# Storing one cast per element in a row, and reading its source with a step of two

## The chip, the cores and the metric

The kernel runs on one core of a Trainium2 chip. The time is that of the device, in microseconds (us), for one execution of the whole program. Three executions of the kernel before took 877.74, 879.22 and 881.9 us; the median is 879.22 us. A core has five engines that the text names: PE (TensorE, matrix products; PEld is its loading of weights), DVE (VectorE), ACT (ScalarE), POOL (GpSimd) and SP (SyncE, which here only issues transfers from memory).

## The reference, cut to what matters

The program computes four residual layers over a sequence of 256 tokens of width 1024 in 32-bit floats, and a last normalisation. Layer 0 and layer 3 are causal pooling mixers, layer 1 is a gated delta rule, layer 2 is latent attention:

```python
for i in range(DEPTH):                     # DEPTH = 4
    kind, j = i % N_MIXERS, i // N_MIXERS  # N_MIXERS = 3
    h = rmsnorm(x, norm_g[i])
    if kind == 0:
        y = pool_mixer(h, pool_w_in[j], pool_w_grp[j], pool_scale[j], pool_w_out[j])
    elif kind == 1:
        y = gdn_mixer(h, gdn_w_in[j], ...)
    else:
        y = mla_mixer(h, positions, mla_w_in[j], ...)
    x = x + y
return rmsnorm(x, final_g)
```

Every mixer is a few large matrix products (`h @ w_in`, products of the mixer's own, `y @ w_out`) with element-wise work between them. Some 137 MB are read from memory, nearly all of it weights, each read once.

## The kernel before, in words

**Products in three parts.** A 32-bit operand `a` of a product is split into `hi`, which is `a` rounded to the type float32r, and `lo`, which is `a - hi`. The product is then `hi*hi + hi*lo + lo*hi`. For weights, `weights` (L110) does this for one row block of 128 x 512 (called a K-tile here): SP loads two K-tiles at a time into one of three `raw` buffers (512 KB, L117), ACT casts `raw` to `whi` (L135; L139 where a gain is multiplied in), and DVE, or in a few K-tiles of layer 1 POOL, writes `wlo = raw - whi` (L136, L140). The pairs go into a ring of nine. A `raw` buffer is free for the next load when both K-tiles in it have been cast and subtracted. For activations `split_out` (L218) does the same with L225/L227 on ACT and L230/L232 on DVE.

**The alternating order.** A product streams one operand through PE (the moving operand, `rhs`) and keeps the other one in it (`lhsT`). `mm` (L148) reads the moving operand in an alternating order: element 0, element n/2, element 1, element n/2 + 1 and so on over each stretch of n columns (`woven`), and writes its result to consecutive columns (`inorder`). So whatever is to be a moving operand has to be stored such that this order gives the true one: the even columns in the first half of the stretch, the odd ones in the second half. The result is as if nothing had been permuted.

**Who stores in it.** There are two kinds of projections in `project` (L156). With `chan` the weights are `lhsT`; their casts read and write in a row. Without it the activations are `lhsT` and the weights move; these casts are called with `weave` and store in the alternating order. Without `chan` go: the first gate and the first mixing of each pooling layer, the gates of layer 1, the first three column blocks of layer 2, its rotary queries and its values, and all four output projections (`layer_out`, L424: first 512 columns at once, then 512 in two cuts of 256). Also stored in that order are the pooled values `ph`/`pl`, the products `yTh`/`yTl` of pooling and attention, the heads' `qkh`/`qkl`/`qk0` (L1246, L1247; read from PSUM, where PE leaves its results), the queries `kqT` of layer 1 (L768), and two small constants (L701, L1107).

In the kernel before such an instruction walks through its operands so that the source is read in a row and every second element is written half a stretch away:

```python
v, lo, hi = inorder(v, weave), woven(lo, weave), woven(hi, weave)
...
a = nc.scalar.copy(hi, v)                              # L135
b = e.tensor_tensor(out=lo, in0=v, in1=hi.bitcast(F32), op=ALU.subtract)  # L136
```

**What sets the order.** Each engine runs its own list of instructions in order and waits by semaphores. The order in these lists is set when the program is built, by a planner that goes by modelled costs. After the last block of an output projection comes a chain that nothing of the next layer can pass: `x` is added up (L429), squares are summed (L239), POOL works out the norm (L275 to L281, L369), the normalised rows `h` (L376, L381) are turned by PE (L396) and split into `hTh`, `hTl` (L225, L230).

Of the kernel before, what the change touches and what calls it, by code (L numbers as in the profile page):

```python
# [16 lines left out]
P = 128  # L17
# [25 lines left out]
def trunk(ctx: ExitStack, tc: tile.TileContext, x, positions, norm_g, pool_w_in, pool_w_grp,  # L43
# [47 lines left out]
    ready = []  # L91
    held_back = {"free": 0, "after": []}

    def inorder(a, n=P):

        if len(a.shape) == 3 and a.shape[2] != n:
            a = a.rearrange("p h s -> p (h s)")
        if len(a.shape) == 3:
            return a.rearrange("p h (a b) -> p h a b", b=2)
        return a.rearrange("p (g a b) -> p g a b", a=n // 2, b=2)  # L100
# [9 lines left out]
    def weights(src, n, cols, raw=None, pool=(), gain=None, weave=0):  # L110

        if raw is None:
            raw = rawp.tile([P, KU * CW], F32, tag="raw", name="raw")
        m = n * cols
        dst = raw[:, :m]
        if len(src.shape) == 3:
            dma = nc.sync.dma_start(out=dst.rearrange("p (k c) -> p k c", k=n), in_=src)  # L117
        else:
            dst = dst.rearrange("p (k a b) -> p k a b", k=n, a=src.shape[2])
            for k in range(n):  # L120
                dma = nc.sync.dma_start(out=dst[:, k], in_=src[:, k])
        parts = []
        for k in range(n):
            v = raw[:, k * cols:(k + 1) * cols]
            lo = ring.tile([P, CW], F32R, tag="wlo", name="wlo")[:, :cols]
            hi = ring.tile([P, CW], F32R, tag="whi", name="whi")[:, :cols]
            parts.append((hi, lo))
            if weave:
                v, lo, hi = inorder(v, weave), woven(lo, weave), woven(hi, weave)
            held = held_back["free"] <= 0  # L130
            held_back["free"] -= 1
            with later(*(held_back["after"] if held else ())):
                e = nc.gpsimd if k in pool else nc.vector
                if gain is None:
# [3 lines that stand above are left out]
                    g = gain[:, k:k + 1]  # L138
                    a = nc.scalar.activation(hi, v, AF.Copy, scale=g)  # L139
                    b = e.scalar_tensor_tensor(out=lo, in0=v, scalar=g, in1=hi.bitcast(F32),  # L140
                                               op0=ALU.mult, op1=ALU.subtract)
        mark.update(sp=dma.ins, act=a.ins)
        if n - 1 not in pool:
            mark["dve"] = b.ins
        return parts
# [72 lines left out]
    def split_out(*tiles, weave=False):  # L218

        if weave:  # L220
            tiles = [(inorder(ps), [woven(o) for o in parts], scale)
                     for ps, parts, scale in tiles]
        for ps, (hi, lo), scale in tiles:
            if scale is None:
                a = nc.scalar.copy(hi, ps)  # L225
            else:
                a = nc.scalar.activation(hi, ps, AF.Copy, scale=scale)  # L227
        for ps, (hi, lo), scale in tiles:
            if scale is None:
                b = nc.vector.tensor_tensor(out=lo, in0=ps, in1=hi.bitcast(F32), op=ALU.subtract)  # L230
            else:
                b = nc.vector.scalar_tensor_tensor(out=lo, in0=ps, scalar=scale,  # L232
                                                   in1=hi.bitcast(F32), op0=ALU.mult,
                                                   op1=ALU.subtract)
        return [a.ins, b.ins]
# [394 lines left out]
    def gdn_layer(i, j, hT):  # L630
# [67 lines left out]
        ps = bank(aux, "aux")  # L698
        nc.tensor.transpose(ps[:M, :P], Gf, ident)
        grow = workb("grow", P)[:M]  # L700
        nc.vector.tensor_copy(woven(grow), inorder(ps[:M, :P]))  # L701
        d_g = dram.tile([M, P], F32, name="d_g")
        nc.gpsimd.dma_start(out=d_g, in_=grow)
        Gb = [big("Gb", H, P) for _ in range(NT)]
# [50 lines left out]
        def channels(dst, c0, hf, which):  # L755
# [4 lines left out]
            for b in range(2):  # L760
                cv = [worka("cv", S) for _ in range(2)]
                conv(*[(banks[b][:, c * S:(c + 1) * S], (c0 + hf * CW) // P + 2 * b + c, cv[c])
                       for c in range(2)])
                for c in range(2):
                    o, v = dst[hf][:, 2 * b + c, :], cv[c]
                    if which:
                        o, v = woven(o), inorder(v)
                    nc.scalar.activation(o, v, AF.Silu)  # L768
            for c in range(0, 4, 2):
                ps = bank(tps, "tp").rearrange("p (t a s) -> p t a s", a=2, t=NT)  # L770
# [325 lines left out]
    def mla_setup():  # L1096
# [5 lines left out]
        for name, src in (("mask16", cmask), ("turn16", ident)):  # L1102
            MC[name] = const.tile([P, P], BF16, name=name)
            o = MC[name]
            if src is ident:
                o, src = woven(o), inorder(src)
            nc.gpsimd.tensor_copy(o, src)  # L1107

    def mla_layer(i, j, hT):
# [123 lines left out]
        def heads(g):  # L1233
            h0 = g * G8
            for c in range(2):
                for dst, w, e, nk, a in ((qT, mla_w_uq[j], 192, NQ, cqT),
# [5 lines left out]
                    for b in range(2):  # L1242
# [1 line left out]
                        two = slice(2 * b, 2 * b + 2)  # L1244
                        split_out((ps[:, :, a0:], [o[:, two] for o in dst[-1][1]], None),
                                  weave=True)  # L1246
                        nc.vector.tensor_copy(woven(dst[-1][0][:, two]), inorder(ps[:, :, :P]))  # L1247
                banks = project(heads_of(mla_w_ukv[j], 256, h0 + 4 * c, 4, NOPE, P), units(NKV),
                                ckn)
                v.append((tuple(big("v" + x, CW, dt=F32R) for x in "hl"), big("v1", CW)))  # L1250
# [138 lines left out]
```

## Time and profile before

| | |
|---|---|
| three executions, median | 879.22 us (877.74 to 881.9) |
| the profiled execution | 880.5 us, span 878.7 us |
| mean granted PE clock in it | 0.973 |
| PE busy | 820.4 us, 93% of the span |
| DVE busy | 700.8 us, 80% |
| ACT busy | 605.6 us, 69% |
| POOL busy | 168.0 us, 19% |
| read from memory | 137.27 MB, 158 GB/s over the span |

The span runs from the first to the last instruction; the 1.8 us beside it belong to the start and the end of the program. A row of the profile names the line of the kernel, the engine, the operation, the written tile and the tiles read (`whi<-raw`), the shape, how often it ran, its busy time and the mean of one. PE's busy time is modelled from pipelined products: a product of 512 columns is shown with 379 ns although the next one starts some 215 ns later, so gaps shorter than the difference don't show as idle time. A row's shape is the product of its dimensions: a cast that stores in the alternating order and one that stores in a row both read 128x512.

### The profile page before, as it was taken

Reading aid. Unit: us, or ns where it says so; the run is one execution under the profiler, and the core shown is the slowest. Engines: PE = TensorE matmul, PEld = TensorE weight load, DVE = VectorE, ACT = ScalarE, POOL = GpSimd, SP = SyncE. Lnnn points to the kernel's source line nnn. Section 1 sums busy time; section 2 is a strip of 40 time slices with the busy share of each in tenths; the row PEclk is TensorE's granted clock in tenths of the full one; section 3 lists DMA queues with packets and bytes.
Section 4 is the critical chain, followed back from the end, with each engine's and each line's share of the span. In section 5 each row is a group of like instructions: output and inputs, shape, how many; then the busy total and the mean of one; then the engine's idle time right before and its main releaser. Section 6 shows DMA issues by size and latency. Waiting matters only on the chain.

```text
span 878.7 us, 16173 instructions
## 1 busy us (share of the span) xinstructions
PE 820.4 (93%) x5962; PEld 768.5 (87%) x5962; DVE 700.8 (80%) x1156; ACT 605.6 (69%) x997; POOL 168.0 (19%) x296
## 2 busy tenths in 40 slices
PE   8989989889899989999979999999999999899995
PEld 6979978878899878888969999999988879899885
DVE  5799889866788978557867789989988867877894
ACT  7676567868765766567867686777866775566784
POOL 3111100141444992023120112000000210000012
PEclk9999989999999989899999999999999999899999
DMA  6755654646655544303637786752542556565463
GB/s 192 224 169 168 192 168 147 198 135 189 187 154 167 167 129 137 121 17 106 183 103 199 226 202 179 203 153 78 168 144 74 167 148 201 160 197 198 139 195 84
DMA packets 109079, 139.90 MB, mean 159 GB/s; under 512 B 21316, under 2 KB 51208, under 8 KB 109000
## 3 DMA queue, kind: packets, MB, share of 16 engines
q1 hardware_dynamic: 106608, 137.12, 52.3%
q0 software_dynamic: 528, 1.58, 0.7%
q8 instruction: 47, 0.77, 0.4%
q10 hardware_dynamic: 1864, 0.17, 0.2%
q14 instruction: 32, 0.26, 0.1%
HBM read 137.27 MB, written 1.58 MB: 158 GB/s over the span
## 4 chain that ended last, share of the span: by engine, by line
PE 49%; DVE 16%; DMA 10%; ACT 10%; issue 7%; POOL 6%; SPq 1%; DVEq 0%; ACTq 0%; POOLq 0%
PE acc L148 38%; DVE wlo L136 7%; ACT whi L135 5%; DMA raw<-in_pool_w_out_dram 4%; PE aux L148 4%; DMA raw<-in_pool_w_in_dram 3%; POOL Tb L831 3%; POOL pr L827 2%; DVE wlo L140 1%; DVE win L531 1%; DVE yTl L230 1%; ACT whi L139 1%; ACT ph L225 1%; PE aux L787 1%; ACT junk L239 1%
## 5 line engine op out<-in xcount | busy, mean ns | idle before, releaser
L135 ACT CAST whi<-raw 128x512 fp32r<-128x512 f32 (+1 forms) x444 | 368.5, 903 | 139.2 <-PE acc L148 50.9
L136 DVE TENSOR_TENSOR wlo<-raw,whi 128x512 fp32r<-128x512 f32 (+1 forms) x430 | 385.0, 949 | 90.3 <-ACT whi L135 87.6
L148 PE MATMUL acc<-hTh,whi 128*128 128x256 f32 x832 | 232.8, 280 | 3.2 <-ACT gsg L651 2.6
L148 PE MATMUL acc<-hTl,whi 128*128 128x256 f32 x832 | 233.0, 280 | 0.0
L148 PE MATMUL acc<-hTh,wlo 128*128 128x256 f32 x832 | 232.0, 279 | 0.4 <-DVE wlo L140 0.4
L148 PEld LDWEIGHTS acc<-hTh,whi 128*128 128x128 f32 x832 | 162.8, 196 | 4.0 <-ACT gsg L651 2.8
L148 PEld LDWEIGHTS acc<-hTl,whi 128*128 128x128 f32 x832 | 162.7, 196 | 0.3
L148 PEld LDWEIGHTS acc<-hTh,wlo 128*128 128x128 f32 x832 | 162.4, 195 | 0.6 <-DVE wlo L140 0.5
L148 PE MATMUL acc<-wlo,yTh 128*128 128x256 f32 (+1 forms) x384 | 116.5, 320 | 8.4 <-DVE wlo L136 8.2
L148 PE MATMUL acc<-whi,yTh 128*128 128x256 f32 (+1 forms) x384 | 114.9, 321 | 4.4 <-ACT whi L135 3.0
L148 PE MATMUL acc<-whi,yTl 128*128 128x256 f32 (+1 forms) x384 | 90.9, 318 | 0.0
L148 PEld LDWEIGHTS acc<-wlo,yTh 128*128 128x128 f32 x384 | 74.4, 194 | 15.8 <-DVE wlo L136 12.5
L148 PEld LDWEIGHTS acc<-whi,yTh 128*128 128x128 f32 x384 | 74.4, 195 | 9.0 <-ACT whi L135 4.2
L148 PEld LDWEIGHTS acc<-whi,yTl 128*128 128x128 f32 x384 | 64.4, 195 | 3.4
L139 ACT ACTIVATE whi<-raw,gain 128x512 fp32r<-128x512 f32 x64 | 47.5, 790 | 28.8 <-DMA raw<-in_pool_w_in_dram 18.5
L364 POOL TENSOR_TENSOR hg<-x,gain 128x256 f32<-128x256 f32 x16 | 14.7, 931 | 264.5 <-DVE x L429 264.5
L148 PE MATMUL acc<-wlo,hTh 128*128 128x512 f32 (+1 forms) x144 | 55.7, 390 | 3.4 <-DVE wlo L136 1.9
L148 PE MATMUL acc<-whi,hTh 128*128 128x512 f32 (+1 forms) x144 | 53.9, 387 | 4.4 <-ACT hTh L225 1.9
L140 DVE SCALAR_TENSOR_TENSOR wlo<-raw,gain,whi 128x512 fp32r<-128x512 f32 x64 | 49.5, 800 | 9.9 <-ACT whi L139 9.7
L148 PE MATMUL acc<-whi,hTl 128*128 128x512 f32 (+1 forms) x144 | 43.0, 377 | 0.1
L530 POOL COPY win<-u 128x4 f32<-128x4 f32 x8 | 6.3, 790 | 180.8 <-ACT u L524 96.5
L148 PEld LDWEIGHTS acc<-whi,hTh 128*128 128x128 f32 x144 | 28.1, 195 | 9.9 <-ACT hTh L225 4.4
(357 smaller groups left out, 1563.5 us busy)
## 6 DMA issues: line engine op xcount, KB each, us to landing
raw<-in_pool_w_in_dram SPq DMA_DIRECT2D x62, 512.0 KB, 4.3
raw<-in_gdn_w_in_dram SPq DMA_DIRECT2D x48, 512.0 KB, 3.9
raw<-in_pool_w_out_dram SPq DMA_DIRECT2D x32, 512.0 KB, 4.3
raw<-in_mla_w_in_dram SPq DMA_DIRECT2D x24, 512.0 KB, 4.6
raw<-in_mla_w_uq_dram SPq DMA_DIRECT2D x36, 256.0 KB, 3.5
raw<-in_pool_w_grp_dram SPq DMA_DIRECT2D x16, 512.0 KB, 3.9
raw<-in_gdn_w_out_dram SPq DMA_DIRECT2D x16, 512.0 KB, 3.7
raw<-in_mla_w_ukv_dram SPq DMA_DIRECT2D x32, 256.0 KB, 3.5
```

The source lines that it names most:

```text
L135: a = nc.scalar.copy(hi, v)
L136: b = e.tensor_tensor(out=lo, in0=v, in1=hi.bitcast(F32), op=ALU.subtract)
L139: a = nc.scalar.activation(hi, v, AF.Copy, scale=g)
L140: b = e.scalar_tensor_tensor(out=lo, in0=v, scalar=g, in1=hi.bitcast(F32), op0=ALU.mult, op1=ALU.subtract)
L148: return nc.tensor.matmul(inorder(o, n), lhsT=lhs, rhs=woven(rhs, n), start=start, stop=stop)
L225: a = nc.scalar.copy(hi, ps)
L230: b = nc.vector.tensor_tensor(out=lo, in0=ps, in1=hi.bitcast(F32), op=ALU.subtract)
L239: nc.scalar.activation(junk[:, :n], src, AF.Square, scale=scale, accum_out=o)
L364: nc.gpsimd.tensor_tensor(out=self.early[t, a], in0=xs[t][:, sl], in1=self.g[:, sl], op=ALU.mult)
L531: nc.vector.tensor_tensor(out=nxt[:, :, d:], in0=cur[:, :, d:], in1=cur[:, :, :S - d], op=ALU.add)
L827: nc.gpsimd.tensor_tensor(out=pv, op=ALU.mult, in0=Lb[:, r, r + 1:, None].to_broadcast([M * Q, n, c]), in1=Tb[:, r:r + 1, :c].to_broadcast ...
L831: mark["blocks"] = nc.gpsimd.tensor_tensor(out=tv, in0=tv, in1=pv, op=ALU.subtract).ins
```

## The change

Two new views, `parted` and `halves`, take the place of `inorder` and `woven` at every instruction on ACT, DVE and POOL that stores in the alternating order. The same elements go to the same places; only the order in which one instruction walks through them is another. Where it went 0, 1, 2, 3 in the source and 0, n/2, 1, n/2 + 1 in the destination, it now goes 0, 2, 4, ... and then 1, 3, 5, ... in the source and 0, 1, 2, 3, ... in the destination. The second source of a subtraction, `hi`, is walked through like the destination. The views of PE (`mm`), of the lower triangle (L794) and of the copies on POOL at L1197 stay.

```diff
+    def parted(a, n=P):
+        if len(a.shape) == 3 and a.shape[2] != n:
+            a = a.rearrange("p h s -> p (h s)")
+        if len(a.shape) == 3:
+            return a.rearrange("p h (a b) -> p h b a", b=2)
+        return a.rearrange("p (g a b) -> p g b a", a=n // 2, b=2)
+
+    def halves(a, n=P):
+        if len(a.shape) == 3 and a.shape[2] != n:
+            a = a.rearrange("p h s -> p (h s)")
+        if len(a.shape) == 3:
+            return a.rearrange("p h (b a) -> p h b a", b=2)
+        return a.rearrange("p (g b a) -> p g b a", a=n // 2, b=2)
@@ weights
             if weave:
-                v, lo, hi = inorder(v, weave), woven(lo, weave), woven(hi, weave)
+                v, lo, hi = parted(v, weave), halves(lo, weave), halves(hi, weave)
@@ split_out
         if weave:
-            tiles = [(inorder(ps), [woven(o) for o in parts], scale)
+            tiles = [(parted(ps), [halves(o) for o in parts], scale)
                      for ps, parts, scale in tiles]
@@ gdn_layer
-        nc.vector.tensor_copy(woven(grow), inorder(ps[:M, :P]))
+        nc.vector.tensor_copy(halves(grow), parted(ps[:M, :P]))
@@ gdn_layer, channels
                     if which:
-                        o, v = woven(o), inorder(v)
+                        o, v = halves(o), parted(v)
@@ mla_setup
             if src is ident:
-                o, src = woven(o), inorder(src)
+                o, src = halves(o), parted(src)
@@ mla_layer, heads
-                        nc.vector.tensor_copy(woven(dst[-1][0][:, two]), inorder(ps[:, :, :P]))
+                        nc.vector.tensor_copy(halves(dst[-1][0][:, two]), parted(ps[:, :, :P]))
```

In the changed file every line behind the new functions has a number that is 16 higher (L136 is L152, L230 is L246).

How the instructions stand shows best on DVE around the output projection of layer 0. The rows give line, operation, what is written from what, and the dimensions of the walk: `128x256x2` is 128 partitions by 256 pairs of elements that lie half a stretch apart. Before:

```order
L136 TENSOR_TENSOR wlo<-raw,whi 128x256x2
L539 SCALAR_TENSOR_TENSOR p<-win,u 128x1024
L136 TENSOR_TENSOR wlo<-raw,whi 128x256x2 x2
L552 SCALAR_TENSOR_TENSOR y<-aux,colsT,gs 128x256 x4
L230 TENSOR_TENSOR pl<-p,ph 128x8x64x2
L136 TENSOR_TENSOR wlo<-raw,whi 128x256x2
L230 TENSOR_TENSOR yTl_1699<-y,yTh_1698 128x4x64x2 x2
L136 TENSOR_TENSOR wlo<-raw,whi 128x256x2 x7
```

And in the change, at the same place:

```order
L152 TENSOR_TENSOR wlo<-raw,whi 128x512
L555 SCALAR_TENSOR_TENSOR p<-win,u 128x1024
L152 TENSOR_TENSOR wlo<-raw,whi 128x512 x2
L568 SCALAR_TENSOR_TENSOR y<-aux,colsT,gs 128x256 x4
L246 TENSOR_TENSOR pl<-p,ph 128x1024
L152 TENSOR_TENSOR wlo<-raw,whi 128x512
L246 TENSOR_TENSOR yTl_1699<-y,yTh_1698 128x512 x2
L152 TENSOR_TENSOR wlo<-raw,whi 128x512 x7
```

Nothing moved here: the same instructions stand in the same order, and the destination is now one run of 512 or 1024 elements. That holds for the whole lists of DVE, ACT, POOL and SP. The one place that moved is on PE, in layer 1, where the third gate's products (L148) run beside the inversion of the triangular blocks (L919). Before:

```order
L148 MATMUL acc<-wlo,hTh_2249 128x512
L148 MATMUL acc<-whi,hTh_2249 128x512
L919 MATMUL aux<-T,LT 128x64 x8
L148 MATMUL acc<-wlo,hTh_2249 128x512
L148 MATMUL acc<-whi,hTl_2250 128x512 x2
```

And in the change:

```order
L164 MATMUL acc<-whi,hTh_2249 128x512
L935 MATMUL aux<-T,LT 128x64 x8
L164 MATMUL acc<-wlo,hTh_2249 128x512
L164 MATMUL acc<-whi,hTh_2249 128x512
L164 MATMUL acc<-wlo,hTh_2249 128x512
L164 MATMUL acc<-whi,hTl_2250 128x512 x2
```

Two products of the gate stand behind the eight small ones instead of ahead of them.

## The prediction

> **What bounds the kernel now.** I read the page first: busy shares, then the chain that ended last.
>
> ```profile
> PE 820.4 (93%) x5962; PEld 768.5 (87%) x5962; DVE 700.8 (80%) x1156; ACT 605.6 (69%) x997; POOL 168.0 (19%) x296
> PE 49%; DVE 16%; DMA 10%; ACT 10%; issue 7%; POOL 6%; SPq 1%; DVEq 0%; ACTq 0%; POOLq 0%
> PE acc L148 38%; DVE wlo L136 7%; ACT whi L135 5%; DMA raw<-in_pool_w_out_dram 4%; PE aux L148 4%; DMA raw<-in_pool_w_in_dram 3%; POOL Tb L831 3%; POOL pr L827 2%; DVE wlo L140 1%; DVE win L531 1%; DVE yTl L230 1%; ACT whi L139 1%; ACT ph L225 1%; PE aux L787 1%; ACT junk L239 1%
> ```
>
> PE is the bound over the whole, but half of the chain runs elsewhere, and the two casts of the weights are its largest part behind the products. So the question is in which stretches PE waits. The view of windows gives PE's busy time in each stretch (first number: its width; then PE, PEld, DVE, ACT, POOL; PEclk is the mean granted clock):
>
> ```profile
> 0.00:23.00 23.00, 19.51 (x81) 15.76 (x82) 13.16 (x17) 16.51 (x25) 7.82 (x61) 1.00 0.64 186
> 43.00:63.00 20.00, 16.23 (x125) 15.38 (x125) 19.36 (x27) 16.24 (x21) 1.39 (x2) 0.93 0.53 163
> 116.00:140.00 24.00, 20.10 (x127) 17.54 (x126) 20.56 (x28) 16.60 (x19) 0.86 (x1) 0.86 0.48 155
> 140.00:184.00 44.00, 40.61 (x268) 37.14 (x267) 34.92 (x40) 30.78 (x38) 6.93 (x10) 0.96 0.62 191
> 184.00:193.00 9.00, 6.39 (x31) 4.28 (x29) 7.04 (x10) 7.52 (x14) 4.30 (x7) 1.00 0.25 62
> 444.00:456.00 12.00, 7.66 (x40) 6.05 (x41) 9.88 (x15) 10.18 (x18) 2.84 (x6) 1.00 0.31 88
> 540.00:600.00 60.00, 60.00 (x489) 58.31 (x487) 54.09 (x107) 44.77 (x86) 3.20 (x2) 1.00 0.60 167
> 640.00:703.00 63.00, 58.05 (x407) 52.63 (x405) 50.39 (x103) 44.82 (x91) 5.53 (x9) 1.00 0.40 126
> 703.00:712.00 9.00, 6.95 (x27) 5.17 (x28) 7.05 (x13) 7.72 (x16) 2.74 (x5) 0.81 0.20 61
> 756.00:770.00 14.00, 10.88 (x68) 10.56 (x67) 11.06 (x16) 7.21 (x11) 2.00 (x3) 0.76 0.55 175
> 817.00:871.00 54.00, 50.51 (x344) 45.94 (x343) 45.58 (x53) 39.12 (x46) 6.57 (x12) 1.00 0.43 140
> ```
>
> Ten of these are stretches whose weights or pooled values are stored in the alternating order; the other, 540 to 600, is the heads of layer 2, where PE has no idle time at all. Without that row PE is idle for 35.1 us (3.5 + 3.8 + 3.9 + 3.4 + 2.6 + 4.3 + 5.0 + 2.1 + 3.1 + 3.5), and the missing clock is worth up to 11.7 us more (the widths times one minus PEclk: 1.4 + 3.4 + 1.8 + 1.7 + 3.4). Idle time understates it, since a product is shown longer than the pitch at which the next starts. The pitch is seen where PE never waits: rows of the timeline for 512 columns, and a piece of the chain for 256:
>
> ```profile
> 530.57 0.38 PE L148 MATMUL acc<-whi,cqT 128*128 128x512 f32 x1
> 530.78 0.38 PE L148 MATMUL acc<-wlo,cqT 128*128 128x512 f32 x1
> 31.61 13.51 PE acc L148 x121
> ```
>
> So 0.215 us for 512 columns (530.78 - 530.57) and 0.112 us for 256 (13.51 / 121). An output projection has 96 products of the first kind and 192 of the second, 20.6 + 21.5 = 42.1 us. In 140 to 184 stand 70 and 192 of them (15.1 + 21.5 = 36.6 us) and a few transposes: about 7 of the 44 us are lost, twice the 3.4 us of idle time.
>
> **What the change does to one instruction.** Of each line a stretch with alternating stores (140 to 183, output projection) and one with stores in a row (720 to 740, `chan`), min/median/max in ns:
>
> ```profile
> L135 ACT CAST whi<-raw x25: 1092/1141/1368, 142.5 to 177.3; 128x512 fp32r<-128x512 f32 x25
> L135 ACT CAST whi<-raw x16: 613/621/625, 721.3 to 737.4; 128x512 fp32r<-128x512 f32 x16
> L136 DVE TENSOR_TENSOR wlo<-raw,whi x27: 1089/1157/1510, 139.6 to 178.4; 128x512 fp32r<-128x512 f32 x27
> L136 DVE TENSOR_TENSOR wlo<-raw,whi x16: 680/688/693, 719.7 to 739.5; 128x512 fp32r<-128x512 f32 x16
> ```
>
> The alternating order costs 520 ns more on ACT and 469 ns on DVE. What no row shows is the new form, a source read with a step of two elements (8 bytes). Lower bound of its price: nothing, 621 and 688 ns. Upper bound from this side: all of it, no gain. Which side is nearer is told by the one operation of the kernel that exists in both orders with only its reading changed: in L794 `LT` reads `DT` in the alternating order, 256 bytes apart, and writes in a row, `attnT` reads in a row.
>
> ```profile
> L794 DVE SCALAR_TENSOR_TENSOR attnT<-aux,rk,DT 128x128 f32<-128x128 f32 x16 | 4.4, 329 | 0.0
> L794 DVE SCALAR_TENSOR_TENSOR LT<-aux,s,DT 128x128 f32<-128x128 f32 x16 | 4.3, 342 | 0.0
> L225 ACT CAST ph<-p 128x1024 fp32r<-128x1024 f32 x8 | 16.4, 2056 | 5.8 <-DVE p L539 5.7
> L230 DVE TENSOR_TENSOR pl<-p,ph 128x1024 fp32r<-128x1024 f32 x8 | 17.2, 2152 | 4.7 <-ACT ph L225 4.7
> L230 DVE TENSOR_TENSOR qkl<-acc,qkh 128x512 fp32r<-128x512 f32 x8 | 9.2, 1149 | 0.5 <-ACT qkh L225 0.5
> L230 DVE TENSOR_TENSOR qkl<-acc,qkh 128x256 fp32r<-128x256 f32 x8 | 5.3, 660 | 0.0
> L1247 DVE COPY qk<-acc 128x256 f32<-128x256 f32 x16 | 10.5, 656 | 0.0
> ```
>
> Reading out of order costs 13 ns per 128 elements, some 50 ns per 512, against the 469 of a subtraction that also writes out of order. So the price sits in the write, and a step of two, a much milder way of reading, should cost between 0 and 50 ns. I take 20 ns: about 500 ns saved per cast, 450 per subtraction, and twice that, 1.0 and 0.9 us, for `ph` and `pl`. By the order, 236 weight casts on ACT, 230 subtractions on DVE and 6 on POOL change; with the activations ACT loses some 145 us of busy time, DVE some 125. Nearly all of it lies under PE's work; only what PE waits for counts.
>
> **What of it lies on the path.** In the output projections a raw buffer goes round: the transfer lands, ACT casts two K-tiles, DVE subtracts, SP issues the next one into it.
>
> ```profile
> SPq L117 <- DVE wlo L136: 30.1, 14, 5.2
> raw<-in_pool_w_out_dram SPq DMA_DIRECT2D x32, 512.0 KB, 4.3
> ```
>
> The first row, waits of SP's queue in 140 to 184, says that all but one of its issues wait for the subtraction. A round is 4.3 + two casts + one subtraction, 7.7 us now (4.3 + 2.28 + 1.16); three buffers give one per 2.58 us, and PE needs 12 x 0.215 = 2.58 us for one. There is no slack, so every `x` addition or `yTl` on DVE in between becomes a gap. With 621 and 688 ns the round is 6.2 us, one per 2.1 us, and a fifth is spare. Transfers then ask for 512 KB per 2.58 us, 203 GB/s; the second of the page's 40 slices (22 to 44 us) shows 224 (row below), so that is there. At the layer ends the chain of waits shows casts inside the sequence that nothing can pass, and at 752 a load of `chan` weights that waits for alternating stores:
>
> ```profile
> 449.06 3.82 ACT whi L135 x4
> 707.52 3.73 ACT whi L135 x4
> 11.00 2.45 ACT whi L139 x2
> 751.06 1.15 DVE wlo L136
> 752.22 4.97 DMA raw<-in_pool_w_in_dram
> GB/s 192 224 169 168 192 168 147 198 135 189 187 154 167 167 129 137 121 17 106 183 103 199 226 202 179 203 153 78 168 144 74 167 148 201 160 197 198 139 195 84
> PE acc L148 <- ACT whi L135: 3.0, 2, 2.6
> ```
>
> Stretch by stretch, against the profiled execution's 880.5 us:
> - 0 to 23: five casts in a row on the chain (two take 2.45 us) shed 2.5 us, of which other arrivals of `x` take some: 1.5.
> - 43 to 63: `ph` sheds 1.0 and two subtractions ahead of `p` 0.9 of PE's 3.8 idle: 2.
> - 116 to 193: lost are 9.9 idle, 5.2 of clock, 1.8 hidden, 16.9 in all. Not recovered: 2.6 (last row above: PE waits for a transfer's cast), 1.6 of the norm chain, half of the clock: 10.
> - layer 1 between: gates and `kqT`, 1. The two products that moved on PE are 0.4 us and wait for nothing else: 0.
> - 424 to 456: four casts shed 2.0 of which 1.6 count, the weights around it 1.4: 3.
> - 640 to 712: 7.0 idle, 1.7 of clock; the attention's own waits stay: 6.
> - 756 to 770: `ph`, `pl` and the casts free the load at 752 some 2.4 us sooner, the half clock costs 1.1 less: 3.5.
> - 817 to 871: 3.5 idle and as much hidden, as in 140 to 184: 4.
> - 540 to 600 and the `chan` parts: 0, since PE covers the casts there in any case; what it costs if that cover goes is the third rival.
>
> The sum is 31 us: 880.5 - 31 = **849.5, say 849 us**. The profiled execution is 1.3 us above the median, which I leave in the range. With all losses recovered (35.1 + 11.7) it would be 834; with half of the sum, 865.
>
> The Trainium skill (Advanced Engine Details and Errata, Memory Cachelines) has a rule for this: lines of 16 bytes in SBUF (the on-chip memory), full rate from two hits per line on, so an fp32 step of two runs at full rate; the sum would be the same. It would also make reading 256 bytes apart slow, which the 342 against 329 ns of `LT` doesn't show. The same section gives PSUM lines of 8 bytes and says that a non-contiguous pattern slows matmuls markedly; if it held for DVE, it would speak against the casts at L1246 and L1247, the third rival.
>
> **The rivals.**
> 1. *The step of two costs what the alternating store cost*, so nothing changes: 880. For it: both walks leave consecutive elements apart, and no row shows ACT reading with a step. Against it: `LT`. 10%.
> 2. *The casts get cheap but half of the gain stays hanging*: at the layer ends the norm chain on POOL, and in the projections DVE's other work, end last; 880.5 - 15 = 865. For it: half of the chain is PE's, and transfers, POOL and issue have 23% of it, which the change doesn't touch. Against it: in the round of 7.7 us the casts are 3.4. 17%.
> 3. *PSUM is slow at a step of two.* `qkh`, `qkl` and `qk` read it; were they twice as dear as now, DVE would get 9.2 + 5.3 + 10.5 = 25 us more (the three rows above) over some 95 us from 540 on, where 54.09 of 60 us are taken, so 10 are free: 15 us later, 864. 5%.
> 4. *Slower: the step of two is dearer than the alternating store*, say by a quarter, 0.29 us per cast. It decides from the first nanosecond, since the round has no slack. Over 236 K-tiles that is 68 us per engine, of which the chain's shares count (7% and 5% of the span, 62 and 44 us, of the busy times below, a sixth and an eighth): 20 us, 900. For it: no row excludes it on ACT. Against it: `LT`, again. 5%.
>
> ```profile
> L135 ACT CAST whi<-raw 128x512 fp32r<-128x512 f32 (+1 forms) x444 | 368.5, 903 | 139.2 <-PE acc L148 50.9
> L136 DVE TENSOR_TENSOR wlo<-raw,whi 128x512 fp32r<-128x512 f32 (+1 forms) x430 | 385.0, 949 | 90.3 <-ACT whi L135 87.6
> ```
>
> 5. *More is recovered*: nearly all idle time and clock go, 835. 8%.
>
> **How the numbers follow.** The forecast has 55%, the rivals 10, 17, 5, 5 and 8. A difference under 0.5% (4.4 us, about what a measurement of this kernel can tell from none) is rival 1 but for a hundredth on either side, with 0.01 for a rival 2 or 3 that eats more than I gave it: 0.10. Slower is rival 4 and that hundredth: 0.06. Faster is the rest: 0.84. The forecast's own range is 841 to 858; 8 in 10 need rivals 2, 3 and 5 as well: 834 to 867.
>
> **What would show it.** `wlo` and `whi` of the output projections near 690 and 620 ns, `ph` near 1.05 us; SP's waits for `wlo` in the output projections mostly gone; PE's idle time in 140 to 184 near 1 us and the four casts at the layer ends near 2.3 us; DVE busy near 575, ACT near 460 us. Wrong would be: casts above 800 ns (rival 1 or 4), `qkl` above 1.15 us with idle PE between 540 and 640 (rival 3), or cheap casts with PE still idle for over 20 us in the stretches above (rival 2).

## The result, and the profile after

The changed kernel takes **831.38 us** (median of four executions, 829.72 to 833.75) against 879.73 us of the kernel before (four as well, 877.74 to 881.9): a ratio of 0.9452, 95% interval 0.9417 to 0.9487. It is 48 us faster. The direction and most places were forecast, the size was not: 849 us was said, and 831 lies below the range of 834 to 867.

The first part of the page of the changed kernel, busy times and shares of the span, and then its chain of waits by engine:

```profile
PE 798.7 (96%) x5962; PEld 756.0 (91%) x5962; DVE 619.1 (75%) x1156; ACT 529.7 (64%) x997; POOL 162.1 (20%) x296
PE 64%; DMA 10%; DVE 9%; POOL 8%; ACT 4%; issue 4%; SPq 0%; POOLq 0%; DVEq 0%; ACTq 0%
```

DVE lost 81.7 us of work and ACT 75.9, and the chain of what ended last now runs through PE for 64% of the span instead of 49%. DVE's share of it fell from 16 to 9%, ACT's from 10 to 4%; DMA kept its 10%, and POOL has 8 instead of 6.

Where the time went shows when each product is looked up in both traces by its place in PE's list (the list is the same but for two products). The view of windows of the changed kernel, over the same stretches of that list as the table of the prediction, in the same order and without 540 to 600 (width; busy PE, PEld, DVE, ACT, POOL; PEclk, DMA share, GB/s); the last row is what lies between 193 and 444 us before, nearly all of it layer 1:

```profile
0.00:21.90 21.90, 19.26 (x82) 15.95 (x83) 11.06 (x17) 14.06 (x25) 6.29 (x60) 1.00 0.62 199
42.00:58.50 16.50, 14.85 (x125) 14.45 (x125) 16.24 (x24) 12.93 (x19) 1.39 (x2) 1.00 0.61 185
111.70:130.00 18.30, 17.11 (x126) 15.57 (x125) 16.97 (x26) 11.99 (x17) 0.63 (x1) 1.00 0.56 185
130.00:167.00 37.00, 37.00 (x269) 35.12 (x268) 24.97 (x39) 24.28 (x39) 6.61 (x11) 1.00 0.69 218
167.00:174.70 7.70, 6.27 (x31) 4.49 (x30) 6.19 (x9) 5.72 (x13) 4.40 (x7) 1.00 0.32 78
418.50:427.30 8.80, 7.71 (x42) 6.10 (x42) 7.39 (x13) 6.91 (x15) 2.15 (x5) 1.00 0.41 116
611.30:666.60 55.30, 55.30 (x407) 52.26 (x406) 38.73 (x92) 35.95 (x86) 6.49 (x10) 1.00 0.44 134
666.60:673.00 6.40, 5.17 (x29) 3.84 (x28) 5.18 (x10) 5.33 (x13) 2.31 (x5) 1.00 0.31 86
717.10:724.90 7.80, 7.80 (x67) 7.67 (x67) 7.80 (x13) 3.44 (x6) 1.25 (x2) 1.00 0.43 139
771.80:819.90 48.10, 48.10 (x344) 45.53 (x342) 33.38 (x51) 30.36 (x46) 5.55 (x10) 1.00 0.50 155
174.70:418.50 243.80, 232.39 (x1670) 217.18 (x1670) 176.69 (x357) 152.99 (x304) 94.59 (x145) 0.97 0.48 147
```

In the three long output projections (rows 4, 7, 10) PE is now busy without a gap, at the full clock: 44.0, 63.0 and 54.0 us became 37.0, 55.3 and 48.1. PE's idle time in the ten stretches is 9.2 us instead of 35.1, and the granted clock, below one in five of them before, is 1.00 in all. DVE, busy for 34.92 of 44 us in the first of these projections, has 12 of 37 us free.

By the same products, the gain of each stretch of the forecast, in us (before and after are one profiled execution each):

| stretch (times of before) | forecast | measured |
|---|---|---|
| 0 to 23 | 1.5 | 1.2 |
| 23 to 63 | 2 | 3.3 |
| 63 to 116 | 0 | -0.1 |
| 116 to 193, output projection of layer 0 | 10 | 14.1 |
| 193 to 424, layer 1 | 1 | 6.2 |
| 424 to 456, layer end | 3 | 4.1 |
| 456 to 640, layer 2 to its attention | 0 | 0.0 |
| 640 to 712, its output projection | 6 | 10.2 |
| 712 to 756, `chan` | 0 | 0.0 |
| 756 to 771 | 3.5 | 6.2 |
| 771 to the end | 4 | 5.5 |
| sum | 31 | 50.7 |

The span goes from 878.7 to 828.0 us, the 50.7 of the table. A further execution of each kernel was profiled. The changed kernel repeats itself: its span is 827.3 us, and no stretch of the table differs from the first profile by more than 1.0 us. The kernel before does so only as a whole: a span of 876.4 us, but with 4.7 us less in 756 to 771, 2.0 less in 640 to 712, 2.9 more at the end and 2.8 more in 193 to 424. So single rows of the table are good to some 3 to 5 us, the sum to some 2 to 3: the medians of all executions give 48.

**What the instruction costs.** The rows of the two cast lines in the output projection of layer 0 of the changed kernel (min/median/max in ns), and the groups of the activations by shape:

```profile
L151 ACT CAST whi<-raw x26: 754/782/931, 131.1 to 166.1; 128x512 fp32r<-128x512 f32 x26
L152 DVE TENSOR_TENSOR wlo<-raw,whi x26: 719/807/1289, 129.3 to 166.9; 128x512 fp32r<-128x512 f32 x26
L241 ACT CAST ph<-p 128x1024 fp32r<-128x1024 f32 x8 | 11.2, 1396 | 3.7 <-DVE p L555 3.6
L246 DVE TENSOR_TENSOR pl<-p,ph 128x1024 fp32r<-128x1024 f32 x8 | 11.1, 1393 | 1.8 <-ACT ph L241 1.8
L246 DVE TENSOR_TENSOR hTl<-tp,hTh 128x512 fp32r<-128x512 f32 x16 | 11.0, 685 | 5.1 <-ACT hTh L241 5.1
L246 DVE TENSOR_TENSOR qkl<-acc,qkh 128x512 fp32r<-128x512 f32 x8 | 5.4, 680 | 0.1
L1263 DVE COPY qk<-acc 128x256 f32<-128x256 f32 x16 | 6.6, 411 | 0.0
```

A weight cast went from 1141 to 782 ns and a subtraction from 1157 to 807: 359 and 350 ns saved, not 500 and 450. So the forecast was too high for what one instruction saves and too low for what the kernel gains. `qkl`, which reads PSUM with the step of two, takes 680 ns, as long as `hTl`, which reads PSUM in a row (685), and as `qkl` itself where it reads in a row (687, in the plain order below).

### The profile page after: what moved, and what is told of

It is laid out like the page before. It is cut to its first block, busy times and chain, and to the rows that moved or that the text cites. A ratio compares the mean times of both kernels' runs of the same rounds, so it can differ in the third digit from the quotient of the medians.

```text
span 828.0 us, 16173 instructions
## 1 busy us (share of the span) xinstructions
PE 798.7 (96%) x5962; PEld 756.0 (91%) x5962; DVE 619.1 (75%) x1156; ACT 529.7 (64%) x997; POOL 162.1 (20%) x296
## 4 chain that ended last, share of the span: by engine, by line
PE 64%; DMA 10%; DVE 9%; POOL 8%; ACT 4%; issue 4%; SPq 0%; POOLq 0%; DVEq 0%; ACTq 0%
PE acc L164 49%; PE aux L164 7%; DMA raw<-in_pool_w_in_dram 3%; POOL Tb L847 3%; DVE wlo L152 2%; POOL pr L843 2%; ACT whi L151 2%; DVE wlo L156 1%; DMA raw<-in_pool_w_grp_dram 1%; DMA raw<-in_gdn_w_in_dram 1%; ACT whi L155 1%; DMA Gb<-d_g 1%; DVE win L547 1%; DMA bw<-in_gdn_w_in_dram 1%; PE aux L976 1%
## 5 line engine op out<-in xcount | busy, mean ns | idle before, releaser
L151 ACT CAST whi<-raw 128x512 fp32r<-128x512 f32 (+1 forms) x444 | 299.2, 710 | 167.1 <-PE acc L164 73.4
L152 DVE TENSOR_TENSOR wlo<-raw,whi 128x512 fp32r<-128x512 f32 (+1 forms) x430 | 313.1, 755 | 113.2 <-ACT whi L151 110.2
L164 PEld LDWEIGHTS acc<-hTh,whi 128*128 128x128 f32 x832 | 160.6, 193 | 2.7 <-ACT gsg L667 2.2
L164 PE MATMUL acc<-wlo,yTh 128*128 128x256 f32 (+1 forms) x384 | 112.5, 311 | 0.7 <-DVE wlo L152 0.7
L164 PE MATMUL acc<-whi,yTh 128*128 128x256 f32 (+1 forms) x384 | 112.2, 315 | 0.0
L155 ACT ACTIVATE whi<-raw,gain 128x512 fp32r<-128x512 f32 x64 | 44.4, 740 | 28.1 <-DMA raw<-in_pool_w_in_dram 20.7
L156 DVE SCALAR_TENSOR_TENSOR wlo<-raw,gain,whi 128x512 fp32r<-128x512 f32 x64 | 47.0, 757 | 9.4 <-ACT whi L155 9.4
L164 PEld LDWEIGHTS acc<-wlo,hTh 128*128 128x128 f32 x144 | 27.6, 192 | 7.5 <-DVE wlo L152 3.1
```

The source lines that it names most:

```text
L164: return nc.tensor.matmul(inorder(o, n), lhsT=lhs, rhs=woven(rhs, n), start=start, stop=stop)
```

## The experiments

Three theories stood against each other at first. A is the prediction's: the round of a raw buffer (transfer, two casts, one subtraction) supplies the output projections, so both casts count alike. B: DVE's list, which runs in order and holds other work as well, is what the products wait for. C, for the activations alone: the long casts inside a sequence that nothing passes.

**The weights alone, and the activations alone.** The new views at `weights` only, and at every other place only:

```diff
# e1_weights_only: before, and
-                v, lo, hi = inorder(v, weave), woven(lo, weave), woven(hi, weave)
+                v, lo, hi = parted(v, weave), halves(lo, weave), halves(hi, weave)
# e2_acts_only: before, and
-            tiles = [(inorder(ps), [woven(o) for o in parts], scale)
+            tiles = [(parted(ps), [halves(o) for o in parts], scale)
...
```

> Only the casts of weights walk in the new order; the activations, kqT and the small constants store in the alternating order as before. Theory A (PE's losses came from weight casts that were late in the output projections and at the layer ends, with a few us more at ph/pl): the stretches of the output projections and layer ends keep their gain, some 15 + 4 + 10 + 5 us, and those at ph/pl (43 to 63, 756 to 770) lose most of theirs: 842 to 847 us. Rival C (the long casts of activations, ph and pl with 2.1 us each, are the late ones that let PE's clock drop): weights alone give no more than half, 855 us or more.

> The opposite: weights store in the alternating order, all activations in the new walk. Theory A: 866 to 872 us, gains only around ph/pl and in layer 1's kqT. Rival C: 855 us or less. If the two parts just add, the gains of this run and of the one with the weights alone sum to 48 us; if a wait is only removed when both are shorter, they sum to less.

Measured: the weights alone 841.14 us (ratio 0.9558, 0.953 to 0.9586), the activations alone 860.0 us (0.9778, 0.9755 to 0.98), against 878.26. (Each experiment is compared with executions of the kernel before that were made beside it: 878.26 us here and for the one-sided runs, 878.11 for the fourth buffer, the casts without a step and the plain order, 878.5 for the filled idle time.) The output projections of layers 0, 2 and 3 with the weights alone, by the same products:

```profile
136.60:173.60 37.00, 37.00 (x268) 35.12 (x268) 25.57 (x38) 24.34 (x38) 6.21 (x10) 1.00 0.67 219
622.30:677.60 55.30, 55.30 (x407) 52.24 (x407) 40.01 (x92) 37.54 (x87) 5.84 (x10) 1.00 0.42 134
783.50:831.60 48.10, 48.10 (x344) 45.53 (x342) 35.80 (x51) 30.87 (x46) 5.56 (x10) 1.00 0.47 156
```

The weights' casts alone bring the three projections to the widths of the whole change (37.0, 55.3, 48.1). Their 37 us and the activations' 18 make 55 us, more than the 48 of both together: a stretch has a floor, PE's own work, and whatever reaches it first takes the gain. The activations' 860.0 lies between what A (866 to 872) and C (855 or less) expected, so their long casts do stand on the path, but not all of them. Where they stand is shown by the same products: in 116 to 140, ahead of the first long projection, the activations alone win 6.0 us and the weights alone 1.3, and in 640 to 703 the activations alone win 4.6.

**One engine's side alone.** The new views on ACT's instructions only, and on those of DVE and POOL only (an instruction's operands all follow its own walk):

```diff
# e3_act_side, in weights: before, and
+                va, ha = parted(v, weave), halves(hi, weave)   # for ACT's cast
                 v, lo, hi = inorder(v, weave), woven(lo, weave), woven(hi, weave)
-                    a = nc.scalar.copy(hi, v)
+                    a = nc.scalar.copy(ha, va)
...
# e4_dve_side: the other way round
+                va, ha = inorder(v, weave), woven(hi, weave)   # for ACT's cast
-                v, lo, hi = inorder(v, weave), woven(lo, weave), woven(hi, weave)
+                v, lo, hi = parted(v, weave), halves(lo, weave), halves(hi, weave)
...
```

> Only ACT's half of each split (hi, and kqT) walks in the new order; DVE's half (lo, qk) stores in the alternating order. Theory A (the round of a raw buffer: landing, two casts, one subtraction): the round falls from 7.7 to some 7.0 us (4.3 + 2 x 0.79 + 1.16), 2.35 per unit against PE's 2.58, so over half of the gain, 850 us. Rival B (DVE's list, 80% busy and in order, is what is late; ACT only waits with it): under a fifth of the gain, 870 us or more.

> Only DVE's half (and POOL's) walks in the new order; ACT's casts store in the alternating order. Theory A: the round is 4.3 + 2.28 + 0.75 = 7.3 us, 2.44 per unit, a little less gain than with ACT's side, 852 us. Rival B: nearly the whole gain, 840 us or less.

Measured: ACT's side alone 854.8 us (0.9724, 0.9706 to 0.9743), DVE's side alone 844.75 us (0.9607, 0.9587 to 0.9627). Again 23.5 and 33.5 us make more than 48. First come the rows of ACT's side alone: the windows of the output projections of layers 0 and 3, and what PE waited for, and for how long, around the first of them:

```profile
134.50:175.90 41.40, 38.55 (x268) 35.38 (x268) 34.54 (x40) 23.06 (x38) 9.60 (x10) 1.00 0.64 203
792.70:846.20 53.50, 51.34 (x344) 47.31 (x342) 44.44 (x52) 29.32 (x46) 8.78 (x10) 0.97 0.43 140
PE acc L167 <- DVE wlo L155: 3.3, 6, 1.0
```

And those of DVE's side alone:

```profile
134.50:174.20 39.70, 38.00 (x269) 35.38 (x267) 25.68 (x38) 30.41 (x38) 6.24 (x10) 1.00 0.64 202
788.00:836.00 48.00, 48.00 (x343) 45.43 (x342) 34.11 (x51) 38.17 (x46) 5.52 (x10) 1.00 0.48 155
PE acc L167 <- DVE wlo L155: 0.6, 2, 0.4
```

With cheap subtractions the last projection is at its floor although each cast of ACT still takes 1142 ns there (1128 in layer 0); with cheap casts and dear subtractions it stays at 53.5 us, and PE goes on waiting for `wlo`. By the round of the raw buffer it should be the other way: a transfer of 4.3 us, two casts and one subtraction make 4.3 + 1.56 + 1.12 = 7.0 us with ACT's side alone and 4.3 + 2.26 + 0.80 = 7.4 with DVE's. A expected the two alike (850 and 852 us), B at least 30 us apart; they are 10 apart, in B's direction. Nearly all of the 10 lies in the three output projections: together they are 161.0 us wide before, 151.8 with ACT's side, 143.1 with DVE's and 140.4 with both. So neither holds alone: both casts count, and DVE's list counts for more than the round says. The kernel before shows the place, in a window inside the first projection and its neighbour:

```profile
110.00:125.00 15.00, 12.02 (x103) 11.38 (x101) 11.56 (x18) 9.20 (x15) 0.00 (x0) 1.00 0.56 176
125.00:140.00 15.00, 13.73 (x73) 11.62 (x73) 15.00 (x19) 11.91 (x12) 0.86 (x1) 0.77 0.33 107
```

From 125 to 140 us DVE is busy for 15.00 of 15 us while ACT has 3 us free: there `p`, `y`, `pl` and `yTl` of the last pooling group stand between the subtractions.

**A fourth raw buffer.** If the round is what limits, another buffer widens it without touching a cast:

```diff
-    rawp = ctx.enter_context(tc.tile_pool(name="rawp", bufs=3))
+    rawp = ctx.enter_context(tc.tile_pool(name="rawp", bufs=4))   # e5: in before; e8: in the change
```

> The kernel before with four raw buffers in place of three; casts unchanged (the planner orders some instructions otherwise with it). Theory A (the round of a raw buffer, 7.7 us for three, is what starves PE in the output projections): a unit comes each 1.93 us, the stretches 116 to 193, 640 to 712 and 817 to the end recover over half of what the change gave there (14 + 10 + 5.5 us): 860 to 866 us. Theory B (DVE's list, in order and with every subtraction 0.45 us longer, is late; the buffers only follow it): 873 us or more.

> The changed kernel with four raw buffers, the control for the planner's other order. Both theories: PE has hardly a gap left in these stretches, so 829 to 834 us. If the other order alone is worth something, it shows here.

Measured: 884.89 us for the kernel before with four buffers (1.0083, 1.005 to 1.0117) and 858.2 for the changed one (0.9779 of before, 0.9741 to 0.9816): both lose, the changed one 27 us. The planner gives a different order with four buffers, and layer 1 pays for most of it (20 of the 27). The second row here is the stretch that takes 251.0 us before and 243.8 after, in the kernel before with four buffers; the others are its output projections of layers 0, 2 and 3:

```profile
133.60:172.30 38.70, 37.60 (x269) 35.32 (x267) 34.41 (x40) 30.00 (x38) 7.05 (x10) 1.00 0.72 217
183.00:455.80 272.80, 240.53 (x1671) 220.65 (x1669) 193.30 (x356) 167.79 (x300) 96.89 (x144) 0.95 0.43 132
655.90:718.40 62.50, 57.99 (x407) 52.36 (x405) 48.77 (x96) 43.42 (x86) 5.50 (x9) 1.00 0.39 120
826.50:876.50 50.00, 48.51 (x343) 45.60 (x343) 44.14 (x51) 38.61 (x46) 6.12 (x10) 1.00 0.44 139
```

And the same stretch of layer 1 in the changed kernel with four:

```profile
176.50:440.20 263.70, 236.93 (x1671) 218.77 (x1670) 175.89 (x357) 150.25 (x301) 93.56 (x144) 0.95 0.44 136
```

So the total decides nothing here. The projections are less disturbed: with dear casts the fourth buffer brings that of layer 0 from 44.0 to 38.7 us and that of layer 3 from 54.0 to 50.0, and does nothing in layer 2 (62.5 for 63.0). So the round may be one limit in the pooling layers and none in layer 2. With the order moved as well this is a hint, not a proof.

**No step at all.** The weights' casts read and write in a row; the output's columns then come out in another order, and nothing else differs:

```diff
# e6_contig: the change, and
             if weave:
-                v, lo, hi = parted(v, weave), halves(lo, weave), halves(hi, weave)
+                pass
```

> The changed kernel, but casts of weights read and write in a row, so the columns of the moving weights come out in another order and the output is not the reference's; work and transfers are the same. It takes away what is left of the price of the step of two (790 against 619 ns on ACT, 751 against 685 on DVE). Theory A (no slack before, slack now): casts near 620 and 690 ns and at most 3 us faster, 828 to 832 us. Rival (time is proportional to cast length, 48 us for 350 and 380 ns): another 12 us, below 822.

Measured: 827.95 us (0.9433, 0.9393 to 0.9474), against the change's 0.9452; the intervals overlap. The two cast rows of its output projection of layer 0, and its busy times:

```profile
L151 ACT CAST whi<-raw x25: 603/618/626, 131.7 to 160.1; 128x512 fp32r<-128x512 f32 x25
L152 DVE TENSOR_TENSOR wlo<-raw,whi x25: 668/692/1215, 129.7 to 161.0; 128x512 fp32r<-128x512 f32 x25
PE 797.8 (97%) x5962; PEld 757.0 (92%) x5962; DVE 603.6 (73%) x1156; ACT 490.0 (59%) x997; POOL 158.4 (19%) x296
```

This gives the step its price in this projection: 782 - 618 = 164 ns per cast on ACT and 807 - 692 = 115 ns per subtraction on DVE. It is no fixed price: in the projections of layers 2 and 3 the same two runs give 782 - 619 = 163 and 847 - 620 = 227 ns on ACT, 755 - 692 = 63 and 783 - 684 = 99 on DVE. Taking away both, some 40 us of ACT's and 16 us of DVE's work, moves the time by some 2 to 3 us, which the overlap of the intervals leaves open. Once PE is the bound in the projections, a cheaper cast is worth almost nothing.

**The plain order everywhere.** What does the alternating order earn, which makes all this necessary? All four views return the operand as it is, and the tokens are loaded, masked and numbered in the order that goes with it:

```diff
# e9_plain_order: the change, and
+        return a
+    halves = inorder = woven = parted
-        return a[0, t * P:(t + 1) * P, :].rearrange("(a b) c -> b a c", b=2)
+        return a[0, t * P:(t + 1) * P, :].rearrange("(b a) c -> b a c", b=2)
...
```

> No alternating order anywhere: tokens are loaded in their own order, everything is stored in a row, and PE reads its moving operand in a row. Casts as in the contiguous case, 620 and 690 ns. If the way in which PE reads its moving operand costs nothing, products keep their pitch of 0.112 and 0.215 us and the time is that of the contiguous case, 828 to 832 us. If reading neighbours in a row is dearer for PE, the pitch grows and with it the time: each 10% of pitch is some 75 us.

Measured: 857.58 us (0.9776 of before, 0.9737 to 0.9816), 26 us more than the change, although every cast reads and writes in a row. The reason is on PE: its busy times, two rows of its timeline and the two long pieces of its chain (start, length, count of products) in the plain order:

```profile
PE 835.4 (98%) x5962; PEld 777.2 (91%) x5962; DVE 603.0 (70%) x1156; ACT 489.9 (57%) x997; POOL 156.7 (18%) x296
520.89 0.40 PE L140 MATMUL acc<-whi,cqT 128*128 128x512 f32 x1
521.12 0.39 PE L140 MATMUL acc<-wlo,cqT 128*128 128x512 f32 x1
434.07 47.65 PE acc L140 x317
693.30 50.44 PE acc L140 x375
```

and the two pieces with the same counts in the change:

```profile
426.39 44.58 PE acc L164 x317
674.57 47.40 PE acc L164 x375
```

In a row, a product of 512 columns starts every 0.23 us instead of 0.215, and the same 317 and 375 products take 6.9% and 6.4% longer. The alternating order of the moving operand is worth its trouble on PE, and the change keeps that while paying less for it at the casts.

**Is the half clock a loss of its own?** Up to the last product the profile of before has 44.4 us of half clock, in nine windows of 3.4 or 6.8 us, that of the change 13.7 in three. Eight of the nine begin after at least 2 us of idle PE in the 6.8 us ahead of them (in a further execution five of eight, the other three after 1.5 to 2.0). Not every such stretch has one: in 444 to 456 PE is idle for 4.3 us at the full clock. If PE runs at half speed for nothing there, up to half of the difference, 15 us, would be the clock's. So two idle stretches of the kernel before were filled with products that nobody reads:

```diff
# e10_filled: before, and
+            if i == 0 and not chan:            # ahead of the first product with ph
+                with later(mark["strip"]):
+                    warming(16)
+                if i == 0 and waiting[0] == 1: # ahead of the first output product
+                    with later(mark["strip"]):
+                        warming(11)
```

> The kernel before, its casts unchanged, with products added whose result nobody reads: 16 small ones (3.4 us by 0.213 us each) on PE ahead of the first product with ph in layer 0, where PE stood idle from 55.9 to 59.7 us and the granted clock fell to one half at 60.2, and 11 (2.3 us) ahead of the first product of layer 0's output projection, idle from 121.9 to 124.5, half clock from 125.1 to 131.9. They fill the idle time and shorten no wait. If the half clock follows from PE's idling and is a loss of its own (theory): both half-clock windows go, PEclk of 43 to 63 and of 116 to 140 is 1.00, and 4 to 5 us (half of 3.4 + 6.8) are won there, so about 874, although only work was added. If PE would have waited for its operands anyway, so that a half clock costs nothing (rival): the clock may rise, but the time stays at 878 or rises by what the added products delay, up to 881. If the windows stay where they were, the half clock doesn't come from the idle time.

Measured: 880.99 us (1.0028, 0.9994 to 1.0062), no change. The windows of its trace at both places, and what PE waited for from 60 to 80 us:

```profile
55.00:60.00 5.00, 4.97 (x43) 4.75 (x42) 4.26 (x6) 5.00 (x7) 0.00 (x0) 1.00 0.49 152
60.00:66.00 6.00, 5.01 (x24) 4.08 (x23) 6.00 (x8) 2.89 (x5) 1.18 (x1) 1.00 0.53 167
125.00:132.00 7.00, 5.73 (x41) 5.08 (x40) 7.00 (x11) 4.91 (x5) 0.00 (x0) 1.00 0.37 128
PE tp L568 <- DVE y L562: 2.9, 1, 2.9
PE acc L148 <- DVE pl L230: 1.0, 1, 1.0
```

In the kernel before the same three windows are

```profile
55.00:60.00 5.00, 1.23 (x10) 1.03 (x9) 4.36 (x6) 5.00 (x6) 0.00 (x0) 1.00 0.50 166
60.00:66.00 6.00, 6.00 (x25) 5.13 (x25) 6.00 (x8) 2.86 (x5) 0.99 (x1) 0.72 0.57 171
125.00:132.00 7.00, 5.73 (x14) 4.08 (x14) 7.00 (x11) 4.83 (x5) 0.86 (x1) 0.51 0.45 150
```

Both half-clock windows are gone (0.72 and 0.51 became 1.00), and a new one stands at 73 us, where PE now waits 2.9 us for `y`: the added products moved a few instructions on DVE, and `y` comes behind `p` there. So at these places the half clock follows the idle time; it does not fall at random. At the first place it was worth little: by the same products this kernel is 0.6 us ahead at 68 us, not the 1.7 of half a window, since PE waits 1.0 us for `pl` instead; DVE is busy for 6.00 of 6 us in both. At the second its worth is not settled: from 110 to 135 us this kernel gains 4.3 us, but it came there 4.2 us late, from the new wait, so its operands had that much more time. The total did not move.

**Both kernels once more**, for where such windows lie in another execution:

> The kernel before once more, for where its half-clock windows lie in another execution. Theory (a window follows a stretch of idle PE): the windows at 60, 125, 176, 705 and 763 us come again at the same places, some 40 to 48 us of half clock in all. Rival (they fall anywhere): other places, other sum.

> The changed kernel once more: theory (windows follow the idle stretches that are left): 10 to 17 us of half clock, in layer 1 (270 to 350 us) and nowhere in layers 0, 2 and 3. Rival: as many windows as in the kernel before, elsewhere.

Single executions of 878.06 and 828.96 us. The kernel before shows 41.0 us of half clock: those near 60, 123, 240, 318 and 369 us come again, those at 176, 292, 705 and 763 do not, and others stand at 342, 448 and 861. The changed kernel has 10.2 us, at 298 and 343, both in layer 1. So some of the places vary from one execution to the next, and the sum differs by 3.4 us, one window, in either kernel. The stretch of `ph` in layer 3, 14.0 us wide with PEclk 0.76 in the profile that the prediction read, is here

```profile
755.60:764.80 9.20, 7.95 (x67) 7.64 (x66) 9.10 (x13) 4.29 (x8) 2.00 (x3) 1.00 0.42 134
```

9.2 us wide at the full clock: most of what the table above gives to this stretch was a loss of that one execution, which another had elsewhere.

## Why the prediction was wrong, step by step

**The bound: right.** The alternating stores held up supply in the ten stretches, PE waited there, and 540 to 600 and the `chan` parts gave nothing (0.0 in both rows). The rivals of a step as dear as, or dearer than, the alternating store are refuted by 782 and 807 ns: the 807 is above the 800 that the prediction had named as their sign, but far below the 1157 that they need; PSUM at a step of two (third rival) by 680 ns for `qkl` and 411 for `qk`. The Trainium skill (Advanced Engine Details and Errata, Memory Cachelines) gives PSUM shorter lines than SBUF. A slowdown of PSUM reads on DVE by that rule is not what these rows show: the step costs nothing there, and costs something in SBUF.

**The price of the step: too low.** "I take 20 ns" was read off `LT`, and the upper end of 50 as well. In the projection of layer 0 it is 164 ns on ACT and 115 on DVE, and `ph` takes 1.40 us instead of 1.05. `LT` is one DVE operation of 128 elements with a PSUM source beside the out-of-order one, and there was no row for ACT at all, so its 13 ns could not carry a bound of 50. DVE ends at 619.1 us and ACT at 529.7, not at 575 and 460. The Trainium skill's rule in the same section (Advanced Engine Details and Errata, Memory Cachelines), full rate from two hits per line, would have given 20 ns or less; the trace does not agree. This error runs against the error of the total, and cost little, since taking the weights' step away altogether won some 2 to 3 us.

**"There is no slack", and the round of the raw buffer: half right.** The row it rested on was SP's waits for `wlo`, 30.1 us in 14 waits in 44 us. The changed kernel, whose PE has no gap in this projection, shows

```profile
SPq L133 <- DVE wlo L152: 24.5, 13, 4.1
```

in 37 us: the same two thirds of the time. The queue waits for a buffer whether or not anyone downstream starves, so the row proves nothing about the bound, and the forecast that these waits would mostly go was wrong with it. DVE's in-order list weighs more than the round, as the two one-sided runs show (844.75 against 854.8 us).

**What of the loss is recovered: the step that failed.** The sum took from each stretch's loss what seemed to stay: 2.6 us of a transfer's cast, 1.6 of the norm chain and half of the clock in 116 to 193; "the attention's own waits stay" in 640 to 712; "as much hidden" only in two places. Measured is that little stayed: the ten stretches together shrank by 44.2 us, where idle time and clock came to 46.8. In 116 to 193 14.1 of the 16.9 came back, not 10. All that the view of waits still shows for PE from 111.7 to 167 us is the first two rows here, 1.2 us in all; the kernel before, from 116 to 184, waited 3.0 us for `whi` and, in the third row, 4.3 for `wlo`:

```profile
PE acc L164 <- DVE wlo L152: 0.7, 1, 0.7
PE aux L164 <- DVE pl L246: 0.5, 1, 0.5
PE acc L148 <- DVE wlo L136: 4.3, 7, 1.2
```

The 2.6 us that the prediction called a transfer's and left standing went as well, and not with the weights: with the weights' casts alone PE still waits 1.8 us for `whi` there, with the activations' alone, or with DVE's side alone, not at all. In the kernel before that transfer starts at 118.04 us, when DVE ends four subtractions that store in a row (115.52 to 118.01); ahead of these in its list stand a `pl` of 2.22 us and two `yTl` of 2.14, which store in the alternating order. So a wait for a transfer can belong to other work further up in the list that frees its buffer. The three projections went to PE's floor: 20.6 us won there (7.0 + 7.7 + 5.9), of which 640 to 703 gave 7.7 with only 4.95 us of idle time, so the loss hidden in products shown longer than their pitch was 2.7 us there, and that term was missing. Such a stretch is no sum of parts: past the point where the supply is faster than PE it is all recovered, before it a part, which is also why the halves of the change add up to 55 and 57 us instead of 48.

Of the 19.7 us between 31 and 50.7, 4.1 lie in 116 to 193, 4.2 in 640 to 712, 5.2 in layer 1, 2.7 in 756 to 771 (where the kernel before had its loss in one execution and not in the other) and 3.5 in the other stretches.

**Layer 1, "1": wrong.** It gave 6.2 us. The row of the kernel before for it is

```profile
193.00:444.00 251.00, 235.87 (x1672) 220.00 (x1670) 191.71 (x354) 169.19 (x299) 99.01 (x144) 0.96 0.48 143
```

beside the last row of the table of windows above: DVE is busy for 15.0 us less, ACT for 16.2 less, and PE's idle time fell from 15.1 to 11.4. The prediction showed no row for this stretch and priced two small items in it. By the same products the weights alone win 2.9 us there and the activations alone 0.4, ACT's side 3.0 and DVE's 4.9. The repeat of the kernel before moves this stretch by some 3 us, so how the 6.2 divide among its waits stays open.

**The layer ends and the first stretch: right.** 3 and 4.1 us at 424 to 456, 1.5 and 1.2 in the first. The four casts in a row at 421 us of the changed kernel take 2.69 us instead of 3.82; 2.3 were forecast, too few by the price of the step.

**The clock.** The forecast counted 2.6 of the 5.2 us in 116 to 193 and 1.1 of the 3.4 in 756 to 770; all five stretches have the full clock now. How much of this is a gain beside the idle time stays open, since the run that filled the idle time had the full clock at two of the places and won nothing in all, with its order on DVE moved a little as well.

The fifth rival, nearly all recovered at 835, with 8%, came nearest: of 35.1 us of idle time 25.9 went, and all of the lost clock. By its own sum it missed the hidden loss, which made up for the idle time that stayed, and layer 1.

## What to carry to other kernels

Where an engine starves behind a supplier that is a little too slow, a cheaper supplier does not save a share of the loss but nearly all of it (here 44.2 us, where 46.8 were counted), as soon as it is faster than the need: take the starved engine's own work as the new width of the stretch, and argue for each microsecond that is to stay above it. Look for the supplier in the windows (an engine busy for 15.00 of 15 us), not in the waits of a queue that always waits for its buffer. When a walk in steps of two cannot be avoided for 32-bit operands, put the step on the reading side, and best where the source lies in PSUM.

## What the runs showed of the hardware

- A step of two on the reading side costs 163 to 227 ns per 128x512 cast on ACT and 63 to 115 ns per subtraction on DVE from SBUF (782 against 618 and 807 against 692 in layer 0), and next to nothing from PSUM (`qkl` on DVE 680 against 687 in a row, `qkh` on ACT 599 against 588). With an alternating store they take 1141 and 1157 ns. The cost of the step is much the same while the other engine still stores in the alternating order: 779 ns on ACT, 799 on DVE.
- PE's products whose moving operand is read in a row take 6 to 7% longer than in the alternating order (47.65 against 44.58 us for 317 products).
- The half clock mostly stands behind some 2 us of idle PE, in windows of 3.4 or 6.8 us, though not behind every such stretch; at two places it went when products that nobody reads filled the idle time (0.72 and 0.51 became 1.00).
